# Weight differences and activation sums of a seven-product feed-forward layer: from GpSimd to VectorE, with their transfers spread and five activation batches fetched ahead

## The chip, the cores and the metric

The kernel runs on one core of one Trainium2 chip. The metric is the device time of one execution in microseconds (us), the median of several runs. A core has five engines that matter here, each with its own queue of instructions that it works off in order: TensorE (PE, matrix products; PEld is its loading of weights), VectorE (DVE), ScalarE (ACT), GpSimd (POOL), and SyncE (SP), which computes nothing and issues nearly all DMA transfers of this kernel. An instruction that waits for a semaphore holds everything behind it on its queue. The planner that builds the program puts the instructions of each queue in an order of its own: it plays the program through on estimated durations and issues what is ready, so an instruction can stand far ahead of its place in the source.

## The reference

One step of an encoder layer, in float32, for a prompt of 2048 rows and a sample group of 128 rows (17 tiles of 128 rows, 1024 columns each):

```python
h = rms_norm(x, norm_g[0]);  z = h @ w_in            # 1024 -> 3592
att = band_attention(...)                            # 8 heads x 64, nine chunks of 64 keys
hb  = mlstm_sequence(...)                            # 4 heads x 128, matrix memory
x = x + rms_norm(concat(att, mlstm_out) @ w_out, norm_g[1])
u = rms_norm(x, norm_g[2]) @ w_up                    # 1024 -> 5632
gate, up = split(causal_conv3(u) + b_conv)
x = x + rms_norm((gelu(gate) * up) @ w_down, norm_g[3])   # 2816 -> 1024
```

Besides y, the outputs are the last keys and values, the memory states and the last columns of u.

## The kernel before, in words

Every float32 product is made of three passes of a reduced type: each operand is split into a high part (ACT copies it, `split` at L1294) and a low part (DVE subtracts, L1295), and `mm3` (L99 to L101) sums high x high, high x low, low x high.

**First phase (about 0 to 1100 us).** The columns of `w_in` are worked off as 14 groups (`GROUPS`, L1180), once for each half of the rows (`seq`, L1216). The loop at L1228 steps through a group's matmuls; at each step it also advances the split of the next group's weights (`load_group`), the norms of the rows (`norm_steps`, one tile of rows at a time: load at L219, square sum, scale at L226, transposes at L71) and two streams of attention and memory work (`pump`). Groups 1 to 12 of the first half also advance `fold_down` (L1161).

**What is folded.** The feed-forward products are not computed as plain products: a product of 2 x 2 blocks is made of seven block products on sums and differences of blocks, instead of eight. For `w_down` the differences T1 to T4 are formed once. `fold_down` does so for 11 rows of blocks in two column pieces each, 22 pieces: a load of 512 KB (L1167), four subtractions of 128 x 256 on GpSimd (L1171 to L1174), a store of 512 KB to the DRAM tensor `wtd` (L1177). The tile is one of the two "xr" buffers, which the row loads use too. Load and store are plain transfers on SP, placed where the planner likes.

**Projection (about 1090 to 1360 us)**, `project`, then the **feed-forward part**: the rows stand in three blocks (`FBLOCKS`) of 6, 6 and 5 tiles; each block has an up stage and a down stage.

**Up stage.** For each of 22 column tiles f (in the order `FORDER`: k, then k + 11) seven products run on PE, their results are combined on DVE (L1582, L1584, L1603, L1458), the convolution runs on ACT and DVE (L1477 to L1479; two small GpSimd copies keep the last columns, L1469 and L1474), GELU and the product of gate and up give the row tile `gt` (L1609). In the first block the differences of `w_up` are also formed on DVE (L1311) and stored (L1313). `store_a` (L1547) stores the quarters of `gt` to DRAM as A11 (at k) and A12, A22 (at k + 11); with both tiles there it forms the sums S1 to S4 in place with four operations of 128 x 384 on GpSimd (L1559 to L1562) and stores them (L1548). The first, third and fourth of these write over a quarter whose store must have landed before.

**Down stage of the first two blocks.** Seven products (`SEQUENCE`, L1357), each over 11 k, take their left operand from these DRAM tensors in batches of two k: six batches a product, 42 in all. `fetch_a(i)` loads batch i: batches 0 and 1 into pairs of "q" buffers (`quad`, 12 of them, which all weight loads use too), the others into "yq" buffers (`row`, 6 of them), which at that time still hold the results of the last column tiles. `split_a(i)` splits it for PE. Batches 0 and 1 are fetched while the up stage still runs; in the down loop step i = 0 fetches 2, 3 and 4, and each later step splits batch i + 1 and fetches batch i + 4. Each batch feeds 18 matmuls of 512 columns. The down stage also loads the rows of the next block into "xr" buffers (L1074, `x2r`), which hold the convolution's inputs `uu` and `ug` until the last convolution is done. The third block has another down stage with 512-column products and fetches its first five tiles early (L1594).

Of the kernel before, what the change touches and what calls it, by code (L numbers as in the profile page):

```python
# [10 lines left out]
F32 = mybir.dt.float32  # L11
F32R = mybir.dt.float32r
AF = mybir.ActivationFunctionType
ALU = mybir.AluOpType
# [3 lines left out]
P = 128  # L18
D = 1024
# [19 lines left out]
HALF = [384, 384, 320]  # L39
PAIRS = [[(((b[j], 0), (b[j + 3], 0)), j * P, P, f"{b[j]}") for j in range(3)] for b in FBLOCKS[:2]]  # L40
NK = NF // 2
FORDER = [f for k in range(NK) for f in (k, k + NK)]
B11, B12, B22, B21 = range(4)
T1, T3, T2, T4 = range(4, 8)
# [4 lines left out]
def hymba_step(ctx: ExitStack, tc: tile.TileContext, I: dict, O: dict):  # L49
    nc = tc.nc  # L50
# [69 lines left out]
    wtd = [dt_([P, 2048], f"wtd{k}") for k in range(NK)]  # L120
# [1037 lines left out]
            nc.scalar.copy(hi, lo.bitcast(F32))  # L1158
            nc.vector.tensor_tensor(lo, lo.bitcast(F32), hi, op=ALU.subtract)

    def fold_down():  # L1161

        for k in range(NK):
            for c in range(2):
                cols = slice(c * 256, (c + 1) * 256)
                t = rows_tile("xr", [P, D], f"fold{k}_{c}").rearrange("p (a n) -> p a n", a=4)
                nc.sync.dma_start(t, I["w_down"][k].rearrange("p (a n) -> p a n", a=4)[:, :, cols])  # L1167
                yield 0.0, 0.0
                yield 0.0, 0.0
                b11, b12, b22, b21 = [t[:, i] for i in range(4)]  # L1170
                nc.gpsimd.tensor_tensor(b11, b12, b11, op=ALU.subtract)  # L1171
                nc.gpsimd.tensor_tensor(b12, b22, b12, op=ALU.subtract)
                nc.gpsimd.tensor_tensor(b22, b22, b11, op=ALU.subtract)
                nc.gpsimd.tensor_tensor(b21, b21, b22, op=ALU.subtract)  # L1174
                yield 0.0, 0.0
                yield 0.0, 0.0
                nc.sync.dma_start(wtd[k].rearrange("p (a n) -> p a n", a=4)[:, :, cols], t)  # L1177
                yield 0.0, 0.0

    GROUPS = ["va0", "qk0", "qk1", "va1", "qk2", "qk3", "qb0", "vo0", "qb1", "vo1", "qb2", "vo2", "qb3", "vo3"]  # L1180
    SRC = {g: i for i, g in enumerate(["va0", "qk0", "qk1", "va1", "qk2", "qk3",
# [37 lines left out]
    chunks = []  # L1219
    norms = norm_steps(0)  # L1220
    next(norms)
    folds = fold_down()
    pend = load_group(0)
    for _ in pend[2]:
        pass
# [2 lines left out]
    for n_, (half, gi) in enumerate(seq):  # L1228
        wh, wl, _ = pend
        split = iter([])  # L1230
        if n_ + 1 < len(seq):
            pend = load_group(seq[n_ + 1][1])
            split = pend[2]
        g = GROUPS[gi]
        i = int(g[2])
        nm = f"{g}_{half}"
        if g[:2] == "va":
            it = group_rows(wh, wl, half, chunks, vd[i], nm, 264 if gi == 0 else 256,
                            [O["v_prompt"][i], O["v_sample"][i].unsqueeze(1)])
        elif g[:2] == "qk":  # L1240
            it = group_T(wh, wl, half, chunks, [qTd[i], kTd[i]], [-(DA ** -0.5), None], nm,
                         [None, [O["k_prompt"][i], O["k_sample"][i]]])
        elif g[:2] == "qb":
            it = group_T(wh, wl, half, chunks, [[t_[:, c, :] for t_ in qkbd[i]] for c in range(2)],
                         [None, DH ** -0.5], nm)
        else:
            it = group_rows(wh, wl, half, chunks, vobd[i], nm)
        if half == 0 and gi == 13:
            chunks = []
            norms = norm_steps(1)  # L1250
        if n_ == len(seq) - 1:
            out = project([0, 1, 2, 3, 4, 5, 6, 7, SAMPLE, 8, 9, 10, 11, 12, 13, 14, 15])
            split = w_out_steps()
            next(split)
            next(out)
        for u, (pe, dve) in enumerate(it):
            ahead = []
            if n_ < len(seq) - 1 or u >= 6:
                ahead.append(next(split, (0.0, 0.0)))
            if n_ == len(seq) - 1 and u == 12:  # L1260
                ahead.append(next(out))
            if (half == 0 and gi == 13 and u >= 6 and u % 2 == 0) or (gi == 0 and u % 2 == 0):
                ahead.append(next(norms, (0.0, 0.0)))
            if half == 0 and 1 <= gi <= 12:
                next(folds, None)
            pump(pe + sum(a[0] for a in ahead), dve + sum(a[1] for a in ahead))
        for _ in split:
            pass
        if gi == 0:
            if half == 0:  # L1270
                nc.sync.dma_start(bgate, I["b_gate"].broadcast_to([P, 8]))
                nc.sync.dma_start(gatt, I["g_att"])
                heads.append(build_bias)
                mems.append(lambda: prep(prep_sample()))
            mems.append(lambda half=half: prep(prep_prompt(half)))
        if g[:2] == "qk":
            attention(i, half)
            if half == 0 and i == 3:
                heads.insert(len(heads) % 4, lambda: attention_sample(0, EARLY))
            if half == 1 and i == 0:  # L1280
                heads.insert(len(heads) % 4, lambda: attention_sample(EARLY, DB))
        if g[:2] == "vo":
            mems.append(lambda i=i, half=half: mlstm(i, half))
            if half == 0:
                mems.append(lambda i=i: mlstm_sample(i))
# [156 lines left out]
    for b, tiles in enumerate(FBLOCKS):  # L1442
        last = b == len(FBLOCKS) - 1
        nt = len(tiles)
        n = HALF[b]
# [71 lines left out]
        def fetch_a(i):  # L1517
            if i >= 6 * len(SEQUENCE):
                return
            p, c = divmod(i, 6)  # L1520
            src = ad[b, SEQUENCE[p][0]]
            ks = slice(2 * c, min(2 * c + 2, NK))
            n_ = (ks.stop - ks.start) * 384
            if i < 2:
                g[i] = [quad(f"ar{b}_{i}_{x}")[:, :384] for x in range(2)]
                for x, r in enumerate(g[i]):
                    nc.sync.dma_start(r, src[:, 2 * c + x, :])
            else:
                g[i] = row(f"ar{b}_{i}")[:, :n_]
                nc.sync.dma_start(g[i], src[:, ks, :].rearrange("p k n -> p (k n)"))  # L1530
# [16 lines left out]
        def store_a(f, gt):  # L1547
# [8 lines left out]
            put("A22", k, second)  # L1556
            gt1 = held.pop(k)
            a11, a21, a12, a22 = gt1[:, 0:384], gt1[:, 384:768], first, second
            nc.gpsimd.tensor_tensor(a11, a11, a21, op=ALU.subtract)  # L1559
            nc.gpsimd.tensor_tensor(a21, a21, a22, op=ALU.add)  # L1560
            nc.gpsimd.tensor_tensor(a22, a22, a11, op=ALU.subtract)
            nc.gpsimd.tensor_tensor(a12, a12, a22, op=ALU.subtract)  # L1562
            for what, src in (("S3", a11), ("S1", a21), ("S2", a22), ("S4", a12)):
                put(what, k, src)

        for fi, f in enumerate(FORDER):
# [23 lines left out]
            if fi == NF - 1:  # L1590
# [5 lines left out]
                else:  # L1596
                    split_a(0)
                    split_a(1)
            ug = u_tile(f"ug{nm}")
            product(P2, w[0], a, onto=True)  # L1600
            nc.scalar.copy(ug[:, 2:2 + n], a[:, :n])
# [20 lines left out]
        if not last:  # L1622
# [47 lines left out]
            for p, (_, _, set_, onto) in enumerate(SEQUENCE):  # L1670
                for c in range(3):
# [8 lines left out]
                    for k in range(4 * c, min(4 * c + 4, NK)):  # L1680
                        i = 6 * p + k // 2
                        if k % 2 == 0:
                            if i == 0:
                                fetch_a(2)
                                fetch_a(3)
                            if i >= 1:
                                split_a(i + 1)
                            fetch_a(i + 4)
                        wk = slice(k % 4 * 512, k % 4 * 512 + 512)
                        ah, al = parts[i]  # L1690
                        for j in range(3):
# [182 lines left out]
```

## Time and profile before

| what | value |
|---|---|
| median of 3 runs | 2834.72 us (2833.73 to 2836.35) |
| the profiled execution | 2845.43 us, its span 2843.6 us |
| PE busy | 2707.8 us, 95% of the span |
| DVE busy | 1942.6 us, 68% |
| ACT busy | 1442.3 us, 51% |
| POOL busy | 628.5 us, 22% |
| DMA | 535.12 MB, mean 188 GB/s |

Times in the rows are from the first instruction on. A row of the waits says who waited for what: total us, how often, the longest. A row of a stretch of time gives the busy time of each engine with the number of its instructions, then the clock that PE was granted (1.00 is full speed), the busy share of the DMA engines and GB/s. A row of a group of instructions ends with busy us and mean ns of one, and then the idle time of its engine ahead of it and what ended that. The profiled execution took 0.4% longer than the median; all sums go against its own rows, and the difference that comes out is taken off the median.

### The profile page before, as it was taken

Reading aid. Unit: us, or ns where it says so; the run is one execution under the profiler, and the core shown is the slowest. Engines: PE = TensorE matmul, PEld = TensorE weight load, DVE = VectorE, ACT = ScalarE, POOL = GpSimd, SP = SyncE. Lnnn points to the kernel's source line nnn. Section 1 sums busy time; section 2 is a strip of 40 time slices with the busy share of each in tenths; the row PEclk is TensorE's granted clock in tenths of the full one; section 3 lists DMA queues with packets and bytes.
Section 4 is the critical chain, followed back from the end, with each engine's and each line's share of the span. In section 5 each row is a group of like instructions: output and inputs, shape, how many; then the busy total and the mean of one; then the engine's idle time right before and its main releaser. Section 6 shows DMA issues by size and latency. Waiting matters only on the chain. (4 is left out here: it accounts for less than half of the span.)

```text
span 2843.6 us, 47569 instructions
## 1 busy us (share of the span) xinstructions
PE 2707.8 (95%) x16389; PEld 2526.5 (89%) x16389; DVE 1942.6 (68%) x3503; ACT 1442.3 (51%) x2916; POOL 628.5 (22%) x1071
## 2 busy tenths in 40 slices
PE   6889999999899999999999997999999899999998
PEld 6789999988799998878889996889999778999877
DVE  4344445655545668766898997757887785888855
ACT  4244545644445666534444445655554565555543
POOL 3231000111100002244332332112232331122220
PEclk9999999999999999999999999999999999999999
DMA  7775446456564556445655556675555696655585
GB/s 233 205 225 181 130 124 184 153 167 184 167 194 127 157 156 191 126 150 188 222 177 170 173 180 217 217 238 163 175 172 159 235 336 222 195 177 168 182 318 188
DMA packets 359025, 535.12 MB, mean 188 GB/s; under 512 B 58787, under 2 KB 196479, under 8 KB 358655
## 3 DMA queue, kind: packets, MB, share of 16 engines
q1 hardware_dynamic: 318270, 491.95, 55.3%
q10 hardware_dynamic: 38592, 33.83, 3.6%
q0 software_dynamic: 1920, 6.29, 0.6%
q8 instruction: 129, 2.11, 0.3%
q14 instruction: 114, 0.93, 0.1%
HBM read 383.87 MB, written 151.21 MB: 188 GB/s over the span
## 5 line engine op out<-in xcount | busy, mean ns | idle before, releaser
L99 PE MATMUL uec<-B,wuh 128*128 128x384 f32 (+1 forms) x720 | 236.5, 330 | 4.7 <-DVE x L1584 1.8
L100 PE MATMUL uec<-B,wuh 128*128 128x384 f32 (+1 forms) x720 | 235.7, 327 | 0.0
L101 PE MATMUL uec<-B,wul 128*128 128x384 f32 (+1 forms) x720 | 234.5, 327 | 0.0
L1294 ACT CAST wuh<-wu 128x512 fp32r<-128x512 f32 x255 | 141.6, 618 | 80.6 <-PE uec L100 75.5
L1295 DVE TENSOR_TENSOR wul<-wu,wuh 128x512 fp32r<-128x512 f32 x255 | 167.5, 695 | 14.5 <-ACT wuh L1294 10.9
L99 PE MATMUL vo<-wi_h,hT 128*128 128x256 f32 x544 | 155.1, 285 | 0.6 <-DVE mt L206 0.6
L101 PE MATMUL vo<-wi_h,hT 128*128 128x256 f32 x544 | 155.6, 286 | 0.0
L100 PE MATMUL vo<-wi_l,hT 128*128 128x256 f32 x544 | 154.8, 285 | 0.0
L400 DVE CUSTOM_DVE_ANT_0 tmp<-s,nb 128x640 f32<-128x640 f32 (+4 forms) x128 | 94.3, 737 | 84.5 <-PE s L390 83.8
L1295 DVE TENSOR_TENSOR wdl<-wdr,wdh 128x512 fp32r<-128x512 f32 x198 | 130.2, 703 | 28.1 <-ACT wdh L1294 25.7
L99 PE MATMUL dn<-wdh,ah 128*128 128x512 f32 x308 | 123.3, 400 | 22.1 <-ACT ah L1294 21.1
L99 PEld LDWEIGHTS uec<-B,wuh 128*128 128x128 f32 x720 | 135.5, 188 | 9.5 <-DVE x L1584 3.1
L99 PE MATMUL qk<-hT,wi_h 128*128 128x384 f32 (+1 forms) x384 | 130.4, 340 | 7.6 <-ACT qk_st L233 4.6
L100 PEld LDWEIGHTS uec<-B,wuh 128*128 128x128 f32 x720 | 135.7, 188 | 0.2
L101 PEld LDWEIGHTS uec<-B,wul 128*128 128x128 f32 x720 | 135.5, 188 | 0.0
L1294 ACT CAST wdh<-wdr 128x512 fp32r<-128x512 f32 x198 | 111.7, 618 | 46.8 <-DMA wdr<-in_w_down 18.7
L413 DVE TENSOR_TENSOR ptl<-pt,pth 128x640 fp32r<-128x640 f32 (+4 forms) x128 | 93.6, 738 | 59.7 <-ACT pth L412 58.8
L401 ACT ACTIVATE tmp<-tmp,mn 128x640 f32<-128x640 f32 (+4 forms) x128 | 97.5, 762 | 67.5 <-DVE mn L400 61.6
L100 PE MATMUL qk<-hT,wi_h 128*128 128x384 f32 (+1 forms) x384 | 129.2, 337 | 0.0
L101 PE MATMUL qk<-hT,wi_l 128*128 128x384 f32 (+1 forms) x384 | 128.7, 335 | 0.0
L100 PE MATMUL qb<-hT,wi_h 128*128 128x384 f32 (+1 forms) x384 | 127.9, 333 | 0.0
L101 PE MATMUL dn<-wdh,al 128*128 128x512 f32 x308 | 124.5, 404 | 2.8 <-DVE al L1295 2.7
(448 smaller groups left out, 9267.0 us busy)
## 6 DMA issues: line engine op xcount, KB each, us to landing
wu<-in_w_up SPq DMA_DIRECT2D x220, 256.0 KB, 3.9
wu<-wsd SPq DMA_DIRECT2D x176, 256.0 KB, 3.8
wdr<-in_w_down SPq DMA_DIRECT2D x110, 256.0 KB, 5.5
wi_raw<-in_w_in SPq DMA_DIRECT2D x52, 512.0 KB, 4.1
wsd<-ws SPq DMA_DIRECT2D x88, 256.0 KB, 3.5
wdr<-wtd SPq DMA_DIRECT2D x88, 256.0 KB, 6.1
ad_S<-g SPq DMA_DIRECT2D x88, 192.0 KB, 1.8
ar<-ad_S SPq DMA_DIRECT2D x40, 384.0 KB, 6.3
```

Of the source, the lines that this page charges most:

```text
L99: nc.tensor.matmul(out, ah, bh, start=start, stop=False, skip_group_check=onto)
L100: nc.tensor.matmul(out, ah, bl, start=False, stop=False, skip_group_check=onto)
L101: nc.tensor.matmul(out, al, bh, start=False, stop=stop, skip_group_check=onto)
L400: nc.vector.tensor_tensor_reduce(o_, s_, b_, 1.0, 3e38, ALU.add, ALU.min, accum_out=mn)
L401: nc.scalar.activation(tmp[:, :n], tmp[:, :n], AF.Exp, bias=mn, scale=-1.0, accum_out=rsum[:, i % 4, hh:hh + 1])
L413: nc.vector.tensor_tensor(s.ptl[:, sl, qc], ptv, s.pth[:, sl, qc], op=ALU.subtract)
L1294: nc.scalar.copy(h, r)
L1295: nc.vector.tensor_tensor(l, r, h, op=ALU.subtract)
```

## The change

It has three parts.

1. The differences of `w_down` are formed on VectorE instead of GpSimd. The 22 pieces have three buffers of their own ("fold") instead of the two "xr" buffers. One piece begins every 12 steps of the first phase's loop, from group 2 to group 12 of both halves, instead of every 5 steps of the first half; its subtractions come 3 steps after the load, its store 2 steps after these. Load and store are pinned behind the transfer that stands before them in the source on SP, so the planner cannot bring them forward past it. (The branch for `down` false is not used.)
2. The four operations of `store_a` run on VectorE instead of GpSimd.
3. Batches 0 to 4 go into "q" buffers. Batches 2, 3 and 4 are fetched during the last column tile of the up stage, behind the splits of batches 0 and 1; the down loop's step 0 fetches nothing.

```diff
+FOLD_STEPS = 12
...
-    def fold_down():
+    def fold_pieces():
         for k in range(NK):
             for c in range(2):
-                cols = slice(c * 256, (c + 1) * 256)
-                t = rows_tile("xr", [P, D], f"fold{k}_{c}").rearrange("p (a n) -> p a n", a=4)
-                nc.sync.dma_start(t, I["w_down"][k].rearrange("p (a n) -> p a n", a=4)[:, :, cols])
-                yield 0.0, 0.0
-                yield 0.0, 0.0
-                b11, b12, b22, b21 = [t[:, i] for i in range(4)]
-                nc.gpsimd.tensor_tensor(b11, b12, b11, op=ALU.subtract)
-                nc.gpsimd.tensor_tensor(b12, b22, b12, op=ALU.subtract)
-                nc.gpsimd.tensor_tensor(b22, b22, b11, op=ALU.subtract)
-                nc.gpsimd.tensor_tensor(b21, b21, b22, op=ALU.subtract)
-                yield 0.0, 0.0
-                yield 0.0, 0.0
-                nc.sync.dma_start(wtd[k].rearrange("p (a n) -> p a n", a=4)[:, :, cols], t)
-                yield 0.0, 0.0
+                yield f"d{k}_{c}", I["w_down"][k], wtd[k], c, True
+
+    def folds():
+        v4 = lambda t: t.rearrange("p (a n) -> p a n", a=4)
+        live = deque()
+        pieces = list(fold_pieces())
+
+        def load(nm, src, dst, c, down):
+            cols = slice(c * 256, (c + 1) * 256)
+            t = v4(pr.tile([P, D], F32, tag="fold", name=f"fold{nm}", bufs=3))
+            tc.keep_in_program_order(nc.sync.dma_start(t, v4(src)[:, :, cols]))
+            live.append((t, v4(dst)[:, :, cols], down))
+
+        def combine(t, dst, down):
+            a, b, c, d = [t[:, i] for i in range(4)]
+            sub = lambda o, x, y: nc.vector.tensor_tensor(o, x, y, op=ALU.subtract)
+            if down:
+                sub(a, b, a)
+                sub(b, c, b)
+                sub(c, c, a)
+                sub(d, d, c)
...
+        for n in range(FOLD_STEPS * (len(pieces) + 1)):
+            i, r = divmod(n, FOLD_STEPS)
+            if r == 0 and i < len(pieces):
+                load(*pieces[i])
+            if (n - 3) % FOLD_STEPS == 0 and 0 <= n - 3 < FOLD_STEPS * len(pieces):
+                combine(*live[-1])
+            if (n - 5) % FOLD_STEPS == 0 and 0 <= n - 5 < FOLD_STEPS * len(pieces):
+                t, dst, _ = live.popleft()
+                tc.keep_in_program_order(nc.sync.dma_start(dst, t))
+            yield
...
-            if half == 0 and 1 <= gi <= 12:
-                next(folds, None)
+            if 2 <= gi <= 12:
+                next(fold, None)
...
+        if n_ == len(seq) - 1:
+            for _ in fold:
+                pass
...
-            if i < 2:
+            if i < 5:
                 g[i] = [quad(f"ar{b}_{i}_{x}")[:, :384] for x in range(2)]
...
-            nc.gpsimd.tensor_tensor(a11, a11, a21, op=ALU.subtract)
-            nc.gpsimd.tensor_tensor(a21, a21, a22, op=ALU.add)
-            nc.gpsimd.tensor_tensor(a22, a22, a11, op=ALU.subtract)
-            nc.gpsimd.tensor_tensor(a12, a12, a22, op=ALU.subtract)
+            nc.vector.tensor_tensor(a11, a11, a21, op=ALU.subtract)
+            nc.vector.tensor_tensor(a21, a21, a22, op=ALU.add)
+            nc.vector.tensor_tensor(a22, a22, a11, op=ALU.subtract)
+            nc.vector.tensor_tensor(a12, a12, a22, op=ALU.subtract)
...
                     split_a(0)
                     split_a(1)
+                    for i in range(2, 5):
+                        fetch_a(i)
...
                         if k % 2 == 0:
-                            if i == 0:
-                                fetch_a(2)
-                                fetch_a(3)
                             if i >= 1:
                                 split_a(i + 1)
-                            fetch_a(i + 4)
+                                fetch_a(i + 4)
```

7 lines of the change are left out of this document (6 added, 1 removed).

## The prediction

> **What bounds the kernel now.** I read the page's totals first, then the stretches of time, then the waits of PE and of SP's queue, and last the DVE groups of the stage that looked full.
>
> ```profile
> span 2843.6 us, 47569 instructions
> PE 2707.8 (95%) x16389; PEld 2526.5 (89%) x16389; DVE 1942.6 (68%) x3503; ACT 1442.3 (51%) x2916; POOL 628.5 (22%) x1071
> ```
>
> PE is the bound: 2843.6 − 2707.8 = 136 us of the span are idle. What the change is worth is therefore the part of these 136 us (and of slow-clock time) that it removes, less what it adds. I looked for where they lie. The first 250 us, and beside them 200 us with the same kinds of groups in the second half of the rows, where nothing is folded:
>
> ```profile
> 0.00:50.00 50.00, 35.19 (x256) 33.85 (x256) 27.42 (x40) 24.33 (x40) 14.59 (x39) 1.00 0.81 246
> 50.00:100.00 50.00, 40.51 (x224) 37.69 (x225) 18.46 (x69) 10.79 (x23) 17.89 (x28) 0.87 0.77 215
> 100.00:150.00 50.00, 37.39 (x209) 35.40 (x207) 12.86 (x28) 14.36 (x35) 12.33 (x17) 0.90 0.70 202
> 150.00:200.00 50.00, 47.14 (x339) 46.66 (x340) 25.16 (x49) 23.69 (x54) 20.55 (x26) 0.97 0.84 248
> 200.00:250.00 50.00, 45.95 (x284) 45.25 (x283) 19.55 (x42) 21.78 (x50) 14.59 (x23) 0.97 0.61 189
> ...
> sum 200.00, PE 184.40 PEld 173.88 DVE 116.29 ACT 92.87 POOL 40.22; mean PE 46.10 PEld 43.47 DVE 29.07 ACT 23.22 POOL 10.05
> ```
>
> The last row is the sum over 550 to 750 us. PE idles 9.5 + 12.6 + 2.9 + 4.0 = 29.0 us between 50 and 250 us, at a granted clock of 0.87 to 0.97, against 200 − 184.4 = 15.6 us there. The queue of SP over the first 260 us tells why:
>
> ```profile
> SPq L1177 <- POOL fold L1174: 39.1, 16, 4.8
> SPq L1167 <- DMA wtd<-fold: 31.4, 16, 3.6
> SPq L1177 <- DMA fold<-in_w_down: 12.0, 5, 3.6
> PE hT_pt L71 <- DVE xr L226: 19.4, 4, 10.3
> ```
>
> SP stands for 39.1 + 31.4 + 12.0 = 82.5 us in the fold's own waits: a store waits for GpSimd's subtractions, the next load for the store of the piece whose buffer it takes. Each wait holds every load behind it. PE's longest wait there, 10.3 us (last row), is for rows that come late.
>
> The two starts of the down stages, and that of the third block, which fetches its tiles early already:
>
> ```profile
> 1710.00:1760.00 50.00, 34.58 (x153) 28.09 (x153) 31.91 (x40) 26.16 (x45) 13.13 (x18) 0.86 0.59 191
> 2230.00:2290.00 60.00, 48.71 (x210) 38.31 (x209) 46.70 (x61) 36.02 (x62) 19.59 (x20) 0.91 0.82 284
> 2680.00:2710.00 30.00, 25.17 (x105) 19.98 (x104) 21.95 (x34) 11.60 (x20) 11.26 (x12) 0.94 0.77 254
> ```
>
> Idle: 15.4, 11.3 and 4.8 us. What PE waits for, and SP's queue at the first start:
>
> ```profile
> PE dn L99 <- ACT ah L1294: 21.1, 2, 11.0
> 1720.28 1.97 SPq L1349 DMA_DIRECT2D wdr<-in_w_down  x4
> 1732.19 0.33 SPq L1074 DMA_DIRECT2D x2r<-x2d  x1
> 1732.55 0.91 SPq L1530 DMA_DIRECT2D ar<-ad_A  x2
> ```
>
> Batches 2 and 3 (L1530) leave only at 1732.55, behind a row load (L1074) that SP could not issue for 9.9 us because its buffer was still in use. So 21.1 us of PE's idle time are two waits for batch 2.
>
> Last, the up stages of blocks one and two:
>
> ```profile
> 1357.00:1711.00 354.00, 330.68 (x1826) 320.29 (x1824) 326.21 (x457) 167.38 (x267) 113.87 (x126) 0.99 0.56 184
> 1899.00:2229.00 330.00, 329.46 (x1878) 327.25 (x1877) 262.33 (x375) 169.01 (x277) 91.88 (x135) 1.00 0.57 174
> ```
>
> In block one PE idles 23.3 us and DVE is busy for 326 of 354 us; in block two PE is full and DVE has 67.7 us to spare. So VectorE, which the change loads, is close to being the bound of one stage and far from it elsewhere.
>
> **The change part by part.**
>
> *Folding leaves the front (gain).* With loads from group 2 on, one piece in 12 steps, three buffers and pinned transfers, the stretch from 50 to 250 us should look like 550 to 750 us: 29.0 − 15.6 = 13.4 us less idle time. The slow clock costs 0.13 x 40.5 + 0.10 x 37.4 + 0.03 x 93.1 = 11.8 us there if the mean holds for the busy part; I take half, 6 us, since the mean also covers idle time. Gain 19 us; bounds 0 (other loads keep the front late) and 13.4 + 11.8 = 25 us.
>
> *Folding on VectorE in the first phase (cost).* 22 x 4 operations of 128 x 256, priced by the same size on DVE:
>
> ```profile
> L656 DVE SCALAR_TENSOR_TENSOR mvo<-mvo,hgm 128x256 f32<-128x256 f32 x32 | 13.5, 423 | 24.7 <-ACT mvo L655 24.4
> 248.00:1100.00 852.00, 829.16 (x6068) 804.48 (x6067) 483.50 (x1198) 457.79 (x1119) 82.69 (x248) 1.00 0.54 160
> ACT wi_h L1201 <- DMA wi_raw<-in_w_in: 23.3, 18, 4.1
> ```
>
> 88 x 0.423 = 37 us, beside a DVE that is idle for 852 − 483 = 369 us: hidden, and uncovered it would cost the 37 us. The subtractions make DVE wait for a load, with the evacuations of PSUM queued behind it. The nearest wait of that kind is ACT's for the weights (between 260 and 1090 us): 18 waits, 1.3 us each. With 22 pieces that is up to 28 us of DVE standing still; ACT's 23.3 us lie in a stretch where PE idles only 852 − 829 = 23 us for all causes, so little of it comes through. I take 3 us; bounds 0 and 15. SP moves 44 transfers of 512 KB past other loads, 11.5 + 11.5 MB over 850 us, 27 GB/s where 160 are moved: nothing, unless a store waits for a late DVE, which is in the bounds.
>
> *Sums of the first block on VectorE (cost).* 11 x 4 operations of 128 x 384. The nearest rows, with those of groups that look slowed, all of block one's up stage:
>
> ```profile
> L1582 DVE TENSOR_TENSOR x<-x,ub 128x384 f32<-128x384 f32 x22 | 12.0, 544 | 0.0
> L1295 DVE TENSOR_TENSOR wul<-ws,wuh 128x512 fp32r<-128x512 f32 x60 | 47.1, 804 | 0.0
> L1479 DVE SCALAR_TENSOR_TENSOR y<-uu,wcv,y 128x768 f32<-128x768 f32 x21 | 25.3, 1205 | 0.1
> L1478 DVE SCALAR_TENSOR_TENSOR y<-uu,wcv,y 128x768 f32<-128x768 f32 x21 | 24.5, 1165 | 2.3 <-ACT y L1477 2.3
> L1295 DVE TENSOR_TENSOR wu<-ws,wu 128x512 fp32r<-128x512 f32 x28 | 21.4, 786 | 0.0
> L1479 DVE SCALAR_TENSOR_TENSOR y<-ug,wcv,y 128x768 f32<-128x768 f32 x20 | 20.2, 1009 | 0.1
> L1311 DVE TENSOR_TENSOR ws<-wu,ws 128x512 f32<-128x512 f32 x21 | 14.3, 680 | 0.0
> L1311 DVE TENSOR_TENSOR ws<-wu,wu 128x512 f32<-128x512 f32 x41 | 28.1, 684 | 17.5 <-DMA wu<-in_w_up 15.9 <-DMA wsd<-ws 1.6
> ```
>
> 44 x 0.544 = 23.9 us more. But equal shapes differ: 512 columns take 680 ns in one group and 804 and 786 in others, 768 columns 1009 and 1205 and 1165. If the long ones are those that ran beside GpSimd's sums, they lose 60 x 0.124 + 28 x 0.106 + 21 x 0.196 + 21 x 0.156 = 17.8 us, which comes back: net 6 us. [...]
>
> Then the waits: the first sum writes over A11, the third over A22, whose stores must land.
>
> ```profile
> L1559 POOL TENSOR_TENSOR g<-g 128x384 f32<-128x384 f32 x11 | 14.2, 1288 | 50.5 <-DMA ad_A<-g 38.3 <-DVE ws L1311 7.7 <-DVE y L1478 4.5
> ad_A<-g SPq DMA_DIRECT2D x66, 192.0 KB, 2.0
> ```
>
> GpSimd stood 38.3 us in them (1357 to 1735 us) at no cost. On DVE the splits of the next weights and the convolution are queued behind, and PE waits for these. Bounds for 22 waits: 0, and 2.0 us each (from issue to landing) = 44 us. DVE's own waits for `wu` (17.5 us) come from loads that its progress frees, and shrink when it has other work meanwhile; so I take 2 us net. With the 6 us above: 8 us, bounds −18 (all contention gone and the 24 us lying in DVE's 28 idle us) and 50.
>
> *Sums of the second block.* 24 us into 67.7 us of DVE's idle time; I take 1 us, bounds 0 and 10.
>
> *Early batches (gain).* Both starts fall to the third block's 4.8 us: 10.6 + 6.5 = 17.1 us. Against it: batch 5 still needs a "yq" buffer and still stands behind the held row load at 1732 us. Batches 2 to 4 cover that:
>
> ```profile
> 1770.00:1780.00 10.00, 10.00 (x47) 8.14 (x46) 7.42 (x13) 7.21 (x14) 0.42 (x1) 1.00 0.79 267
> ```
>
> 47 matmuls in 10 us, so 54 give 11.5 us of work, about the longest wait of 11.0 us. I take 16 us; bounds 0 and 21.1 plus 4 of slow clock. Ten "q" buffers of 12 could delay weight loads; the third block does the same and shows 4.8 us.
>
> The sum: −19 + 3 + 8 + 1 − 16 = −23 us. Against the profiled execution that is 2845.4 − 23 = 2822; this stands 10.7 us above the median of the runs, from which I take the same 23: 2834.7 − 23 = **2812 us**.
>
> **The rivals.**
>
> *VectorE waits for the stores and becomes the bound of the first up stage.* For it: DVE has 28 idle us there, 17.5 of them such waits. Against: the planner sees the landing and can place the sums later. At 2.0 us a wait the term is 6 + 44 = 50 instead of 8: 2834.7 − 23 + 42 = 2854 us. It decides from (23 + 2) / 22 = 1.1 us a wait, where the gain is gone. [...]
>
> *The front is late for other reasons* (the bias rows that are spread over all partitions, the weights), and the fold's waits only fill time: 2834.7 − 4 = 2831 us. For it: DMA is busy 0.70 to 0.84 there; against: 82.5 us of SP in the fold's waits.
>
> *The early fetches do not come early*, because "q" buffers or the planner hold them, or batch 5 becomes the new wait of the same length: 2834.7 − 7 = 2828 us.
>
> *All of it goes well*: front 25, starts 21, up stage 0, other costs 0: 2834.7 − 46 = 2789 us.
>
> **How the numbers follow.** Chances: the forecast 0.52, VectorE's waits 0.14, the front 0.12, the fetches 0.13, all well 0.09. The range 2790 to 2842 us holds all but most of the first rival and half of the last, 0.8. The forecast's own range is 2803 to 2822 us. A measurement of this kernel can tell 0.2% (5.7 us) from no change: faster means below 2829. That is 0.51 of the forecast, 0.09 of all well, 0.08 of the fetches' case and 0.03 of the front's, 0.71 together; slower 0.14 of VectorE's waits and 0.02 of the front's, 0.16; the same 0.13.
>
> **What would show it.** Right: PE's idle time from 50 to 250 us near 16 us at a clock near 1.00, no row of SP waiting in the fold; the waits of `dn` for `ah` gone and idle time at both starts near 5 us; in block one's up stage no DVE group of 512 columns above 720 ns. Wrong: rows of DVE `g` waiting for the DMA `ad_A<-g` with more than 25 us in sum and an up stage longer than 362 us; or DVE `fold` waiting for its load with PE's idle time from 250 to 1100 us well over 23 us.

## The result, and the profile after

The changed kernel takes 2807.89 us (median of 4 runs, 2806.88 to 2809.64) against 2835.34 us for the kernel before on the same chip: a ratio of 0.9904, 95% interval [0.9887, 0.9922], 27.4 us faster. The forecast of 2812 us was close. The terms behind it were not: two of the five were far off, in opposite directions, and cancelled.

First the totals of the profile after (its profiled execution took 2809.64 us):

```profile
span 2807.9 us, 47466 instructions
PE 2707.0 (96%) x16389; PEld 2524.4 (90%) x16389; DVE 1971.0 (70%) x3685; ACT 1441.0 (51%) x2922; POOL 474.9 (17%) x895
```

PE works as long as before (2707.0 against 2707.8 us); its idle time falls from 135.8 to 100.9 us. Part of that is the profile of before, which stands 10 us above the median of its runs; so the spans of the two traces differ by 35.7 us where the medians differ by 27.4, and in what follows a stage's difference is read within a few us.

To see where the time went, both traces are cut at the same pieces of work. The boundaries are the start of the second half of the rows (group "va0" for the second time), and then the starts of block one's up stage, its down stage, block two's up stage and its down stage. The columns are: stretch, length, busy time of PE, PEld, DVE, ACT and POOL, clock, DMA share, GB/s. Before:

```profile
0.00:556.30 556.30, 509.84 (x3533) 497.77 (x3534) 263.42 (x598) 256.02 (x583) 102.79 (x200) 0.97 0.60 178
556.30:1357.20 800.90, 775.69 (x5173) 714.25 (x5172) 503.56 (x1101) 417.23 (x1024) 156.68 (x310) 1.00 0.55 166
1357.20:1711.20 354.00, 330.48 (x1825) 320.10 (x1824) 326.41 (x458) 167.58 (x268) 114.07 (x126) 0.99 0.56 184
1711.20:1899.10 187.90, 172.26 (x761) 140.03 (x762) 127.57 (x182) 111.02 (x197) 25.84 (x34) 0.96 0.67 219
1899.10:2218.90 319.80, 319.27 (x1831) 318.72 (x1829) 253.28 (x364) 164.51 (x271) 88.33 (x130) 1.00 0.58 177
2218.90:2404.20 185.30, 173.28 (x761) 139.08 (x762) 138.96 (x194) 108.30 (x194) 48.35 (x56) 0.97 0.78 269
```

And after:

```profile
0.00:530.10 530.10, 505.47 (x3532) 495.27 (x3533) 274.90 (x642) 255.79 (x584) 33.68 (x112) 0.98 0.53 165
530.10:1347.20 817.10, 783.90 (x5174) 719.11 (x5173) 514.99 (x1144) 417.15 (x1024) 161.02 (x309) 0.99 0.57 177
1347.20:1689.60 342.40, 326.64 (x1825) 318.69 (x1823) 319.29 (x495) 168.18 (x268) 80.66 (x86) 0.99 0.58 188
1689.60:1864.60 175.00, 170.96 (x761) 138.49 (x761) 129.92 (x192) 111.17 (x200) 24.57 (x29) 1.00 0.72 239
1864.60:2186.00 321.40, 319.81 (x1830) 318.41 (x1828) 263.70 (x404) 163.39 (x271) 41.47 (x90) 1.00 0.56 175
2186.00:2366.60 180.60, 173.75 (x761) 139.31 (x762) 140.26 (x201) 108.09 (x197) 41.00 (x52) 0.98 0.82 278
```

The lengths differ by −26.2, **+16.2**, **−11.6**, −12.9, +1.6 and −4.7 us, and the third block by +1.9. The front gained more than the forecast said, the second half of the first phase with the projection gave 16.2 of it back, block one's up stage became shorter where it was to become longer, and the two down stages went as forecast.

**The front.** Stretches of the same length as in the prediction:

```profile
50.00:100.00 50.00, 43.91 (x247) 41.28 (x246) 20.23 (x82) 13.97 (x32) 0.58 (x4) 0.97 0.57 175
100.00:150.00 50.00, 47.05 (x332) 46.32 (x332) 19.20 (x47) 21.16 (x55) 1.18 (x3) 0.93 0.62 177
150.00:200.00 50.00, 50.00 (x335) 49.79 (x334) 25.38 (x51) 25.42 (x55) 0.58 (x4) 1.00 0.45 136
200.00:250.00 50.00, 50.00 (x312) 49.51 (x311) 24.32 (x55) 23.30 (x54) 0.00 (x0) 1.00 0.46 141
```

PE idles 6.1 + 2.9 = 9.0 us there instead of 29.0. SP's queue over the first 260 us, longest sums first:

```profile
SPq L448 <- DVE attst L444: 25.0, 3, 9.3
SPq L1220 <- DVE wi_l L1227: 22.9, 7, 8.1
```

Neither is the fold's; of its 82.5 us of waits two rows with 0.6 and 0.9 us are left. What SP waits for now are a result of the attention that it stores (L448) and the buffers for the group's weights (L1220).

**Block one's up stage.** Groups of DVE there, with the idle time ahead of each at the end of the row:

```profile
L1323 DVE TENSOR_TENSOR wul<-ws,wuh 128x512 fp32r<-128x512 f32 x60 | 39.9, 689 | 0.0
L1323 DVE TENSOR_TENSOR wu<-ws,wu 128x512 fp32r<-128x512 f32 x28 | 18.7, 688 | 0.0
L1506 DVE SCALAR_TENSOR_TENSOR y<-uu,wcv,y 128x768 f32<-128x768 f32 x21 | 21.3, 1016 | 3.1 <-ACT y L1505 3.1
L1587 DVE TENSOR_TENSOR g<-g 128x384 f32<-128x384 f32 x10 | 5.6, 555 | 0.0
L1339 DVE TENSOR_TENSOR ws<-wu,wu 128x512 f32<-128x512 f32 x41 | 28.3, 690 | 11.5 <-DMA wu<-in_w_up 10.0 <-DMA ad_S<-g 1.5
```

512 columns cost 687 to 690 ns in every group, where the groups of before had 680 to 804. 768 columns of the convolution cost 1016, where 1009 to 1205 stood. The four sums (L1587 is one of them) cost 555 ns each, and no wait for `ad_A` stands ahead of them.

**The down stages.** SP's queue around the first start (start, length in us, what it issues):

```profile
1677.34 4.29 SPq L1555 DMA_DIRECT2D ar<-ad_A  x6
1712.09 0.33 SPq L1075 DMA_DIRECT2D x2r<-x2d  x1
1712.47 0.90 SPq L1558 DMA_DIRECT2D ar<-ad_A  x2
```

The six transfers of batches 2 to 4 leave 12 us before the stage starts (1689.60). The next batch still leaves behind the row load at 1712.09, but PE has work until then: its waits for `ah` fell from 21.1 to 0.7 us, and the first 50 us of both stages look like this:

```profile
1688.00:1738.00 50.00, 46.68 (x213) 37.24 (x212) 41.81 (x64) 33.40 (x60) 7.59 (x12) 1.00 0.74 245
2184.00:2244.00 60.00, 53.51 (x234) 42.76 (x233) 51.00 (x72) 36.10 (x64) 15.83 (x21) 0.94 0.80 279
```

3.3 us idle where 15.4 stood, and 6.5 where 11.3 stood.

### The profile page after: what moved, and what is told of

Same layout as the page of the kernel before. It is cut to its first block, busy times and chain, and to the rows that moved or that the text cites. A ratio compares the mean times of both kernels' runs of the same rounds, so it can differ in the third digit from the quotient of the medians.

```text
span 2807.9 us, 47466 instructions
## 1 busy us (share of the span) xinstructions
PE 2707.0 (96%) x16389; PEld 2524.4 (90%) x16389; DVE 1971.0 (70%) x3685; ACT 1441.0 (51%) x2922; POOL 474.9 (17%) x895
## 5 line engine op out<-in xcount | busy, mean ns | idle before, releaser
L101 PE MATMUL qb<-hT,wi_h 128*128 128x384 f32 (+1 forms) x384 | 128.3, 334 | 0.0
L100 PE MATMUL qb<-hT,wi_h 128*128 128x384 f32 (+1 forms) x384 | 127.6, 332 | 0.0
```

The source lines that it names most:

```text
L100: nc.tensor.matmul(out, ah, bh, start=start, stop=False, skip_group_check=onto)
L101: nc.tensor.matmul(out, ah, bl, start=False, stop=False, skip_group_check=onto)
```

## The experiments

Two questions followed. Each of the three parts should have a price of its own; and something takes back 16 us after the front: the subtractions on VectorE, the transfers of the fold, or their places in the queues. In the results a ratio is to the kernel before on the same chip, with its 95% interval. The kernel before took 2835 to 2842 us on the chips used, so versions are compared by their ratios and not by their times.

**The parts one by one.** `fold_only` is the change without its parts 2 and 3; `sums_only` and `early_only` are the kernel before with one part.

```diff
 # sums_only, in store_a (and its three sister lines)
-            nc.gpsimd.tensor_tensor(a11, a11, a21, op=ALU.subtract)
+            nc.vector.tensor_tensor(a11, a11, a21, op=ALU.subtract)
 # early_only (and the last hunk of sums_early, below)
-            if i < 2:
+            if i < 5:
...
+                    for i in range(2, 5):
+                        fetch_a(i)
```

> Part 1 alone: folding on VectorE, spread and pinned; the sums stay on GpSimd and the early batches are undone. My theory (the parts work in different stages and add): the front gains as in the changed kernel (second group va0 at about 530 instead of 556 us), the rest of the first phase and the projection lose about 16 us (801 to 817 us), the up and down stages stay at 354, 188, 320 and 185 us: about 2825 us, 10 us faster than before. Rival A (the 16 us have nothing to do with the fold but with the shifted order of another part): the rest stays at about 801 us and the time is about 2810. Rival B (the front's gain was an accident of one profiled execution): no change, about 2835 us.

> Part 2 alone: the four sums of a column tile on VectorE. Theory from the result (VectorE loses more to GpSimd's sums than it takes to do them itself): the up stage of block one falls from 354 to about 342 us and that of block two stays at about 320: about 2824 us. My prediction had it 8 us slower there (about 2843 us), because of waits for the stores of A11 and A22. Rival (the up stage is faster in the changed kernel only since early batches free something): no gain, 2835 us or a little above.

> Part 3 alone: batches 0 to 4 in q buffers, fetched in the last column tile. Theory: both waits of dn for ah (11.0 and 10.0 us) go, the down stages fall from 187.9 and 185.3 to about 176 and 179 us: about 2818 us, 17 us faster. Rival (the rows free earlier only because the sums are done sooner on VectorE, so part 3 alone is held by the row load on SP): half of it or less, 2827 us or more.

Measured: the fold alone 2849.29 us, 1.0032 [1.002, 1.0045], so not a gain; the sums alone 2837.63 us, 0.9984 [0.9974, 0.9995]; the early batches alone 2820.99 us, 0.9939 [0.9926, 0.9951]. The first two stretches of the fold alone (up to the second half, and from there to the up stage), and then block one's up stage with the sums alone:

```profile
0.00:531.00 531.00, 502.87 (x3533) 490.36 (x3534) 273.95 (x641) 255.06 (x584) 33.59 (x112) 0.99 0.54 164
531.00:1351.70 820.70, 786.71 (x5173) 721.27 (x5172) 515.30 (x1145) 417.16 (x1023) 159.83 (x310) 0.99 0.57 177
```

```profile
1354.50:1699.10 344.60, 328.87 (x1825) 320.47 (x1823) 319.55 (x495) 168.81 (x268) 85.84 (x86) 0.99 0.59 188
```

The fold alone repeats the picture: 556.3 − 531.0 = 25.3 us won in the front, 820.7 − 800.9 = 19.8 us lost until the up stage. Its trace is 2.3 us shorter than that of before, while its timed runs are slower; they spread from 2840 to 2856 us, wider than those of any other kernel, the profiled one is the second fastest of the ten, and I have no cause for that. The sums alone shorten their stage from 354.0 to 344.6 us, but the kernel by some 4.5 us only, not to the 2824 us expected. The early batches by themselves bring 17 of the 27 us. By the ratios the three parts come to +9 − 5 − 17 = −13 us one by one, where the whole brings −27: they do not simply add up, against the theory behind these runs.

**The change without its first part.** This is the kernel before with parts 2 and 3, run beside the changed kernel as it is.

```diff
 # sums_early: before.py with the two edits above, and
-                            if i == 0:
-                                fetch_a(2)
-                                fetch_a(3)
                             if i >= 1:
                                 split_a(i + 1)
-                            fetch_a(i + 4)
+                                fetch_a(i + 4)
```

> Parts 2 and 3 without part 1: folding as before, on GpSimd in the front. Theory so far: part 1 gives 25 us in the front and gives most of it back in the first phase's second half and the projection, so its own worth is near nothing. Then the stages are 133, 423, 801 us up to the up stage as before, then 342 to 345, 174, 320 and 180 us, and the time is within 6 us of the changed kernel's (about 2810 us). Rival (part 1 is worth the 10 us that its trace of the whole change shows): 2817 us or more.

> The changed kernel once more, on the chip and in the rounds of the others, so that they are compared with it directly: about 0.990 of the kernel before, and stages as in its first profile within 4 us each.

Measured on the same chip: without part 1 2809.40 us, 0.9893 [0.9878, 0.9909]; the changed kernel 2813.74 us, 0.9905 [0.989, 0.992]. The intervals overlap: **the first and largest part of the change brings no gain that can be measured,** and alone it even cost 9 us. Parts 2 and 3 bring 30 us together, where they brought 22 one by one; why that is so was not followed up. The same two stretches, first without part 1:

```profile
0.00:550.70 550.70, 508.88 (x3532) 497.64 (x3533) 264.81 (x598) 255.93 (x583) 102.75 (x200) 0.97 0.60 179
550.70:1348.70 798.00, 778.04 (x5174) 718.36 (x5173) 504.43 (x1101) 417.70 (x1024) 155.74 (x310) 0.99 0.54 167
```

and with it:

```profile
0.00:531.60 531.60, 504.07 (x3533) 492.67 (x3534) 274.53 (x641) 255.59 (x584) 34.71 (x112) 0.99 0.54 164
531.60:1356.60 825.00, 786.54 (x5173) 721.87 (x5173) 515.67 (x1145) 417.84 (x1024) 161.14 (x310) 0.99 0.57 176
```

Part 1 reaches the second half 19.1 us earlier and needs 27.0 us longer from there to the up stage. Of these 27.0 us, 18.5 are PE's idle time (38.5 against 20.0 us) and 8.5 are matmuls that take longer (786.5 against 778.0 us busy for the same matmuls). The other traces say the same: the four kernels that fold as before reach the second half at 550.7 to 558.6 us and the up stage at 1348.7 to 1361.7 us, the four with part 1 as it stands (the changed kernel twice, the fold alone, and the one without the sums, below) at 530.1 to 531.6 and 1347.2 to 1356.6 us.

**What gives the front's gain back.** Five versions of the fold, all else as in the changed kernel: no fold at all (`no_fold`: the down stage reads plain `w_down` for all blocks); its transfers without the subtractions (`fold_copy`); the subtractions on GpSimd (`fold_gpsimd`); the subtractions four steps later (`late_combine`); the transfers not pinned (`not_pinned`).

```diff
 # no_fold (and the loop that runs the rest of the pieces behind the last group goes too)
-                next(fold, None)
+                pass
...
-            src = I["w_down"][k] if blk < 4 else wtd[k]
+            src = I["w_down"][k]
 # fold_copy
-                combine(*live[-1])
+                pass
 # fold_gpsimd
-            sub = lambda o, x, y: nc.vector.tensor_tensor(o, x, y, op=ALU.subtract)
+            sub = lambda o, x, y: nc.gpsimd.tensor_tensor(o, x, y, op=ALU.subtract)
 # late_combine (and n - 5 -> n - 9 for the store)
-            if (n - 3) % FOLD_STEPS == 0 and 0 <= n - 3 < FOLD_STEPS * len(pieces):
+            if (n - 7) % FOLD_STEPS == 0 and 0 <= n - 7 < FOLD_STEPS * len(pieces):
 # not_pinned (and the store in the same way)
-            tc.keep_in_program_order(nc.sync.dma_start(t, v4(src)[:, :, cols]))
+            nc.sync.dma_start(t, v4(src)[:, :, cols])
```

> The changed kernel without any fold: no load, no subtraction, no store, and the down stages read w_down's own blocks where the differences belong (same sizes; this leaves part of the computation out). Question: where do the 16 us come from that the stretch from the second half's first group to the up stage (801 us before) gained? If the fold's own work causes them, this stretch is back at about 801 us and the time about 2790 us. If they come from the order of the other work (the front is faster, the streams are cut differently), it stays at 812 us or more, and the time near 2803 us.

> The changed kernel with the fold's loads and stores but without its 88 subtractions (this leaves part of the computation out). If VectorE's standing still for the fold's loads is what costs, this is like having no fold, about 801 us in that stretch and 2792 us in all. If it is the 44 transfers of 512 KB and their pinned places on SP's queue, it stays near 812 to 817 us and 2805 us.

> The changed kernel with the fold's subtractions back on GpSimd; spread, buffers and pinned transfers stay. If the front's gain is that of the spread and the pinned transfers, the front is as in the changed kernel (second va0 at about 530 us). If the 16 us lost later in the first phase come from VectorE standing still for the fold's loads (47.1 us of such waits), they fall to about 5 us and the time is about 2800 us. If the engine does not matter, about 2808 us. If moving to VectorE was what helped, it is slower than 2812 us.

> The changed kernel with the subtractions 7 steps behind the load instead of 3, and the store 9 instead of 5. If VectorE's waits for the loads (47.1 us) cost the time, they fall below 10 us and the time to about 2798 us, as with GpSimd. But if the planner sets the subtractions by its own estimate of the landing, the waits stay near 40 us and the time near 2808 us.

> The changed kernel without the pins: the planner may bring the fold's loads and stores forward past other transfers, as far as the three buffers let it. If the pins (not the 12 steps) keep the fold out of the front, the front is slow again: second va0 at 545 us or later and 2825 us or more. If the spread over the loop alone does it, within 5 us of 2808.

Measured: no fold 2779.94 us, 0.9784 [0.9769, 0.9798]; transfers without subtractions 2810.03 us, 0.9892 [0.9876, 0.9909]; on GpSimd **2798.30 us, 0.9863 [0.9847, 0.988]**; four steps later 2813.03 us, 0.9902 [0.9888, 0.9917]; not pinned 2812.97 us, 0.9904 [0.9889, 0.9919]. The stretch from the second half to the up stage, one row from each, in this order:

```profile
519.10:1319.50 800.40, 776.66 (x5174) 715.99 (x5173) 503.03 (x1099) 417.13 (x1024) 155.03 (x309) 1.00 0.54 166
```

```profile
523.90:1343.30 819.40, 784.89 (x5190) 720.38 (x5190) 504.38 (x1107) 418.68 (x1030) 163.22 (x318) 1.00 0.58 178
```

```profile
528.40:1341.20 812.80, 782.49 (x5191) 721.54 (x5190) 512.98 (x1107) 418.79 (x1027) 196.70 (x362) 0.99 0.59 179
```

```profile
530.50:1354.10 823.60, 787.29 (x5173) 723.87 (x5172) 516.57 (x1144) 416.84 (x1024) 157.75 (x309) 0.99 0.57 176
```

```profile
541.40:1351.30 809.90, 780.56 (x5150) 717.09 (x5149) 496.34 (x1093) 414.54 (x1013) 154.02 (x306) 0.99 0.53 162
```

The copy without one subtraction still needs 819.4 us there, against 800.4 without the fold. On one chip the times are 2810.03 against 2779.94 us. So nearly all of the fold's cost is there without the subtractions and without DVE's waits for their loads, although these waits exist. The version on GpSimd does take the 2800 us that its expectation named for the case that these waits cost the time, but that is no proof of it: its stretch is 812.8 us instead of about 806, and the copy, which has no such waits either, is not measurably faster than the changed kernel. All operations of the tile `foldd` and what they waited for, in the changed kernel:

```profile
L1182 DVE TENSOR_TENSOR foldd<-foldd x88: 365/424/427, 74.7 to 880.4; 128x256 f32<-128x256 f32 x88
  DMA foldd<-in_w_down: 47.1, 20
```

and the waits with the subtractions four steps later:

```profile
  DMA foldd<-in_w_down: 40.5, 21
```

47.1 us in 20 waits, 2.4 us each. Four steps more of the source's order hardly change that, as was expected for the case that the planner places the subtractions by its own estimate of the landing; so this run did not take the waits away, and only `fold_copy` decides.

What the copy has and `no_fold` has not are 44 transfers of 512 KB and their places in SP's queue. But these cannot be the whole of it either. Not pinned, the planner brings the whole fold forward into the first 160 us:

```profile
L1182 DVE TENSOR_TENSOR foldd<-foldd x88: 404/424/630, 15.5 to 156.5; 128x256 f32<-128x256 f32 x88
```

The front is then late again (541.4), but there is no transfer of the fold left in the second half, and the stretch still takes 809.9 us, 9 to 12 us more than without part 1 (798.0) or without the fold (800.4). That is near the scatter of single traces, since the changed kernel itself took 817.1 and 825.0 us there in two executions; but these 809.9 us also hold 23 matmuls fewer than the 800.9 us of before.

The planner orders all queues anew for every version, and in one place what this does can be counted. From the last matmul of the last group (`vo`) to the up stage, before and after:

```profile
1087.60:1357.20 269.60, 264.57 (x1424) 221.62 (x1424) 191.15 (x300) 132.20 (x315) 99.94 (x133) 1.00 0.49 161
1067.50:1347.20 279.70, 270.99 (x1456) 225.19 (x1455) 193.53 (x313) 135.25 (x325) 101.21 (x138) 1.00 0.48 158
```

The changed kernel does some 30 matmuls more there, attention and memory work that stood further ahead before, and needs 10.1 us more: 6.4 of work and 3.7 of idle time. The fold's last store has left SP at 913.04 us, 154 us earlier. This stretch takes 269.4 to 270.7 us in all versions with the old fold or none, 279.3 to 283.4 us in those with the spread fold, 292.0 us not pinned (14.6 of them idle), and 270.2 us in the simple version on GpSimd, the fastest of those that fold. So 10.1 of the 16.2 us appear where the fold has nothing to do any more. But 6.4 of these are work that was moved there: counted where that work stood before, some 12.5 us are lost while the fold is at work and 3.7 us behind it. Not pinned, PE idles 9.6 us more than before there and 5.4 us less ahead of it, 900 us behind the fold's last transfer: an order of the queues alone moves its idle time by several us.

One wait before that can be followed. The waits from 750 to 775 us in the changed kernel:

```profile
POOL mb L681 <- DMA mb<-md: 24.0, 2, 20.3
DVE spl L899 <- ACT sph L898: 9.9, 1, 9.9
ACT w L697 <- POOL mb L681: 7.7, 1, 7.7
PE sot L100 <- ACT sph L898: 3.8, 1, 3.8
```

The loads of `mb`, a small tile of the memory part, leave SP at 761.43 us. GpSimd waits 20.3 us for them, ACT 7.7 us for GpSimd with the high parts of other operands queued behind it, and DVE and PE wait for those. What holds the loads back is not shown: a store of the fold leaves SP shortly before, at 758.35 us, but its 0.58 us on SP are little, and the order of the queue around it is another one too. The clock suffers too. Below are the 10 us that hold PE's wait in the changed kernel, the next 10, and the 10 us that hold the same wait in the copy, where it is 2.6 us long:

```profile
760.00:770.00 10.00, 6.17 (x42) 5.83 (x42) 0.32 (x1) 1.63 (x4) 0.81 (x2) 0.96 0.31 96
770.00:780.00 10.00, 10.00 (x50) 9.26 (x50) 6.26 (x11) 6.02 (x13) 1.83 (x5) 0.86 0.71 200
760.00:770.00 10.00, 7.45 (x33) 6.65 (x32) 3.50 (x6) 4.24 (x10) 1.61 (x5) 0.83 0.51 146
```

A wait of PE stands near this place in the other versions too. It is 3.6 to 4.2 us with the fold alone, without the sums, on GpSimd and in both executions of the changed kernel, 2.7 us not pinned and 5.0 us, at a neighbouring matmul, four steps later; but with the old fold or none it is 1.8 to 2.9 us as well. So this is one place of a few us, clock included. For the rest of the 12 us I found no single wait that stands in the versions that lose and not in the others.

**On GpSimd, later.** From group 4 on, one piece in 10 steps:

```diff
 # fold_gpsimd_later: fold_gpsimd, and
-FOLD_STEPS = 12
+FOLD_STEPS = 10
...
-            if 2 <= gi <= 12:
+            if 4 <= gi <= 12:
```

> The best so far (the changed kernel with the fold's subtractions on GpSimd) with the fold begun two groups later (from group 4 of both halves) and one piece in 10 steps instead of 12. Without any fold the second va0 starts at 519 us, with it at 528 to 530: if the fold's transfers in the first groups cause that, it comes near 522 us and the time near 2793 us. If a fold transfer costs the same wherever it lies, about 2799 us.

Measured: 2804.05 us, 0.9873 [0.9855, 0.9891]. The front is 2 us shorter (526.2 against 528.4, not the 522 of the first case), the rest is not. It is no better than the simple version on GpSimd, and the two intervals overlap.

**What the sums cost on VectorE.** The changed kernel with the four operations left out:

```diff
-            nc.vector.tensor_tensor(a11, a11, a21, op=ALU.subtract)
-            nc.vector.tensor_tensor(a21, a21, a22, op=ALU.add)
-            nc.vector.tensor_tensor(a22, a22, a11, op=ALU.subtract)
-            nc.vector.tensor_tensor(a12, a12, a22, op=ALU.subtract)
```

> The changed kernel without the four sums of a column tile (S1 to S4 are stored as the plain quarters; this leaves part of the computation out), on no engine at all. If VectorE is still the bound of block one's up stage, the stage falls further, from 342 towards the 327 us that PE is busy; block two's stays at 320. If the stage is now bound by something else (PE, the loads), it stays at 340 to 342 us, and the sums on VectorE cost nothing any more.

Measured: 2801.12 us, 0.9867 [0.9852, 0.9881]. Block one's up stage, and the wait of DVE there:

```profile
1351.00:1686.60 335.60, 323.80 (x1825) 319.81 (x1823) 303.41 (x458) 167.94 (x268) 75.13 (x87) 0.99 0.60 194
```

```profile
DVE ws L1339 <- DMA wu<-in_w_up: 17.8, 16, 1.9
```

Without the sums the stage takes 6.8 us less, between the two expected cases, for 15.9 us less work on DVE; the waits for `wu` grow from 10.0 to 17.8 us. DVE's free time there is partly made of these waits, and 9.1 of the 15.9 us went into it (32.2 us idle without the sums, 23.1 with them). So by these traces the sums cost 6.8 us of this stage on VectorE and 6.8 + 11.6 = 18.4 us on GpSimd, although nothing but DVE's slower instructions showed it. (The whole kernel is 12.6 us faster than the changed one on the same chip; the rest of that lies in other stretches.)

## Why the prediction was right, and where it was not

**The front** (−19 predicted, bounds 0 and 25): right in its cause, a little small. PE's idle time from 50 to 250 us is 9.0 us, where 16 were expected, and the second half starts 26.2 us earlier in the trace, 19.1 us in the pair on one chip. The rival of a front that is late for other reasons falls: with the whole fold back in the front (not pinned) the second half starts at 541.4 us, without any fold at 519.1.

**Folding on VectorE in the first phase** (+3 predicted, bounds 0 and 15): **this step failed.** It measured +16 (the profile after), +20 (alone) and +24 (817.1, 820.7 and 825.0 against 800.9), outside its bounds. The mechanism I bounded, DVE standing still for the loads, is there with 47.1 us, where up to 28 were counted, and is not the main cause; a copy without subtractions loses 18.5 us as well. I had priced the moved transfers at nothing, by their share of the traffic. That is the term that was wrong: with them and without a single subtraction the kernel takes 30 us more than without a fold. How they cost it is in part open. They come with a new plan for the whole second half, which moves work behind the fold's end and leaves 3.7 us more idle time there; that the rest are places in the queues ahead of small transfers, on which a chain of ACT, DVE and GpSimd hangs, is argued and not shown. The sign that I named for it, PE's idle time from 250 to 1100 us, did come: 850 − 820.6 = 29.4 us instead of 23.

```profile
250.00:1100.00 850.00, 820.60 (x5941) 791.95 (x5939) 503.07 (x1248) 448.92 (x1101) 90.19 (x254) 0.99 0.58 179
```

Even that reading misses most of it: half of the loss is slower matmuls (PE's busy time rose by 8.2 of the 16.2 us for the same work), which idle time does not show, and a part lies in the projection behind 1100 us.

**The sums of block one** (+8 predicted, bounds −18 and 50): **the second step that failed**, in sign. The stage became 11.6 us shorter. The mechanism was right, and both sizes were not. DVE's busy time fell by 7.1 us (326.41 to 319.29) although 38 sums came into the stage. The run without them is busy for 303.41 us: so the sums add 15.9 us, where 23.9 were counted for all 44, and 23.0 us came back, where 17.8 were counted. (A sum has 555 ns of its own and adds less, since the records of neighbouring DVE instructions overlap: the one that starts at 1458.69 us in the changed kernel lasts 0.55 us, and the next instruction starts 0.47 us after it did.) I had counted the four groups that looked slowest (17.1 us of it); others, with less to see in their means, were slowed as well. Two of them in the kernel before, which came down to 687 and 1016 ns:

```profile
L1311 DVE TENSOR_TENSOR ws<-ws,wu 128x512 f32<-128x512 f32 x21 | 16.0, 760 | 0.0
L1478 DVE SCALAR_TENSOR_TENSOR y<-ug,wcv,y 128x768 f32<-128x768 f32 x21 | 22.7, 1080 | 0.0
```

And DVE's idle time fell by 4.5 us (27.6 to 23.1), where I had added 2 for waits: the two differences make the 11.6. That the long instructions were those beside GpSimd's sums was an assumption when I priced them, which no row of the forecast showed. The trace of before shows it, instruction by instruction. In block one's up stage a subtraction of 512 columns took 0.67 to 0.69 us where no sum ran on GpSimd and up to 1.52 us beside one (at 1535.86 us), a convolution instruction of 768 columns 1.00 to 1.02 us and up to 1.83 us (at 1521.51 us); the groups with one input in PSUM took 0.54 to 0.56 us either way. With the sums on VectorE 804 and 786 ns became 689 and 688 (682 in both groups with the sums alone), and the groups with one input in PSUM, 544 to 547 ns before, took 551 to 552. The rival of the stores did not come: no sum waits for a landing, as the argument against it had said.

**The sums of block two** (+1): 319.8 to 321.4 us in the profile after, with 10.4 us more on a DVE with room. Right.

**The early batches** (−16): 12.9 + 4.7 = 17.6 us in the trace, −17.3 us by the ratio for the early batches alone. Right in the mechanism, in the size, and in what covers batch 5: the row load still holds the queue, and PE does not notice.

So the sum of −23 met 27.4 by luck in two terms: +3 was +16 to +24, and +8 was −12. That the time came out as forecast says nothing for or against the chances of the rivals. None of them described what happened, a first part that takes its gain back further on.

## What to carry to other kernels

When work is moved out of a crowded stretch into one with slack, do not price the moved transfers by their share of the traffic, and measure the stretch that receives them, and the ones behind it, since here they gave back what the crowded one had gained. What the transfers stand in front of in their queue, and what new order the planner makes of the rest, are the things to look at next. In a stage that VectorE nearly fills, elementwise work on GpSimd can be paid for by the VectorE instructions that run beside it (here the mean of 60 subtractions of 512 columns fell from 804 to 689 ns when it went, while the groups with an input in PSUM stayed near 550): compare the mean of equal shapes in all groups, not only in the slowest. Where VectorE has slack and GpSimd stands idle, the same move can be wrong: the fold on GpSimd, spread as here, with the sums on VectorE, gave the fastest full kernel of this study, 2798.30 us (0.9863, clear of the 0.9904 of the changed kernel, not of 0.9873 and 0.9893 in two other versions).

## What was not expected

- The fold of `w_down` costs 22 to 34 us in all its forms (0.9784 without it against 0.9863 on GpSimd, 0.9893 as it was before, 0.9904 in the changed kernel), although its subtractions are 37 us on an engine that idles 837 us in the changed kernel (2807.9 − 1971.0) and its traffic is 23 MB of 535.
- The clock fell after short waits of PE: after 3.8 us in the changed kernel (0.86 in the next 10 us) and after 2.6 us in the copy (0.83 in the 10 us that hold the wait), but not after 2.6 us in the kernel before (1.00 from 778 to 788 us). With 2.6 us in both of the last two, the length of the wait alone does not tell whether the clock falls.
- What exactly costs the rest in the second half stays open. The runs exclude the subtractions as the only cause (`fold_copy`). The presence of the transfers in that half cannot be the only one either: without them (`not_pinned`) the stretch is still 9 us longer than before, with 23 matmuls fewer in it, though that is near the scatter of single traces. That a new order of the queues costs the remainder is argued, not shown. Nor was it tested whether the fold's transfers slow the others on the DMA engines; the loads of the first phase's weights (`wi_raw`) land in 4.5 us (median) in the kernel before and in the changed one, but both have these transfers.
